# A fourth buffer for weight chunks in the FFNs of a fp32 encoder trunk, and FFN operands without the mixer's row factor

## The chip, the core and the metric

The kernel runs on one core of one Trainium2 chip. The metric is the device time of one launch in microseconds. Five engines work side by side, each on its own list of instructions in order: TensorE (PE, matmuls; PEld, its weight loads), VectorE (DVE), ScalarE (ACT), GpSimd (POOL) and SyncE (SP). Here SP and POOL do little but issue DMAs. An instruction waits on semaphores for what it needs, and everything behind it on its engine waits with it.

## The reference, cut to what matters

Two layers; in each a half-step FFN, a mixer (short convolution and chunk-band attention, gated) and a second half-step FFN; a final RMSNorm. 512 prompt frames and 8 x 16 sample frames make 640 columns.

```python
def _rmsnorm(x, g):
    y = x * lax.rsqrt(jnp.mean(x * x, axis=-1, keepdims=True) + EPS)
    return y * g

def _swiglu(h, w_gu, w_down):
    g, u = jnp.split(h @ w_gu, 2, axis=-1)          # 1024 -> 2 x 2816
    return (jax.nn.silu(g) * u) @ w_down            # 2816 -> 1024

for l in range(2):
    x = x + 0.5 * _swiglu(_rmsnorm(x, norm_ffn1[l]), w_ffn1_gu[l], w_ffn1_down[l])
    x = x + _mixer(_rmsnorm(x, norm_mix[l]), ...)
    x = x + 0.5 * _swiglu(_rmsnorm(x, norm_ffn2[l]), w_ffn2_gu[l], w_ffn2_down[l])
y = _rmsnorm(x, norm_final)
```

## The kernel before

**Layout.** x stays on the chip as 8 tiles of 128 channels by 640 columns (`x[0..7]`), in two halves of 320 columns (`HT`). Each fp32 product is made of three matmuls in a reduced fp32 form (fp32r): an operand z is split into `hi`, the rounded copy (a cast by ScalarE), and `lo = z - hi` (VectorE), and hi·hi, lo·hi and hi·lo are summed in PSUM (`multiply`, `block`).

**Weights.** They come from HBM as one stream of 379 chunks of 128 x 1024 (512 KB), `wst`, in the order of use. `load(n)` issues the DMA of chunk n on SP into a tile `raw`; the pool has three of them, so that the load of chunk n waits until chunk n-3 has been read for the last time. `prep` splits a chunk into `whi` (ScalarE, L296) and `wlo` (VectorE, L301), three buffers each. `source` makes, for the products in seven steps, sums of weight blocks (`add`, L240): first `s<-raw` and `s<-s,raw` (from the second chunk rb of a unit, and the first, ra), later `raw<-raw,raw` and `raw<-s,raw`. A unit of two chunks gives four slabs in this way. `ahead()` and `begin()` place these steps in the program in advance of the products that use them; `pending` and `flush` hold back the `lo` parts.

**FFNs.** There are four: a0, b0, a1, b1 (a before, b after the mixer of a layer; `FFNS` gives their chunks of the 22 blocks of hidden channels). `gate_up` makes one block of g and u by the seven-step scheme (`pa`, `pb`, `pc` are PSUM banks, `c_` tiles copies of them by ScalarE, called c1, u2 and c5 and held in the tag `cap` of the FFN's pool `fp`, five buffers). `down_rows` makes four output rows of the down projection of a chunk of four blocks, again in seven steps X11, X21, N6, T5, T7, 22, T4: `a` is a bank that is taken twice (after T7 by VectorE, `x<-daa` or `x<-dab`, L982; then T4 is accumulated into it and it is taken again), `b` is taken once (`x<-dba`). Other parts are staged by ScalarE into `cap` tiles (`c_a`, `u_a`) and added into x by accumulating DMAs from POOL (L977). The last chunk of an FFN goes by plain products (`pda`, `pdb`). The first blocks of a0 are made by `opening`, while x still arrives.

**Norms.** The class `Expand` makes the next FFN's operands, while the products before it still run: `final(m)` follows the last update of `x[m]`. It squares x[m] (ScalarE), multiplies x[m] by the gain g (and, in b0, a1 and b1, by the factor `rr` of the norm before, L518 on VectorE; in a0 there is none, and ScalarE does it, L516), forms sums and differences of the halves (`xe`, `xo`) and splits them. The norm's own factor `rho` isn't known yet; it is applied later to the products of the gates. With the factor `rr` in the operands, `rho` has to be the ratio of two norms: `diagonal` multiplies by `prev.s` (L587), and `inverse` makes the new `rr` (L603, in b0 alone). `total`, `root`, `diagonal` and `spread` follow in the first `gate_up`: matmuls sum the squares across channels (`nps`, L464), ScalarE takes the root, VectorE the inverse, and matmuls spread it again (`nbc`, L593).

**The room.** `sp` is a small pool that lives through the whole kernel. Its tag `rr` has two buffers of 640 columns, used by the mixer's norm (`caps` and `rr`), by `inverse`, by two tiles of `opening` and by `Final`. The pool `fp` belongs to the FFNs; it is closed before a mixer and opened again at its end. The mixer's pools `yp`, `op`, `mp` and `gp` take the same room meanwhile.

**Order.** TensorE's order is that of the program. Within `manual_schedule(engines=ORDERED)` that holds for VectorE and ScalarE too; from the block `free` of an FFN on up to its `cut`, the scheduler places VectorE's and ScalarE's instructions by its own estimate of when they are ready. SP's and POOL's queues are in order.

Of the kernel before, what the change touches and what calls it, by code (L numbers as in the profile page):

```python
# [16 lines left out]
P = 128  # L17
# [37 lines left out]

ROWS = (1, 2)

XT4, XN6, XT7, X21, X22, X11, XT5 = range(7)
# [64 lines left out]
def kinds():  # L123


    out = []

    def plain(n):
        out.extend([8] * (n // 8) + [n % 8] * (n % 8 > 0))
# [33 lines left out]
    return out  # L163

# [10 lines left out]
def trunk(ctx: ExitStack, tc: tile.TileContext, xin, wst, small, pbias, samplebias, kcache, vcache,  # L175
# [44 lines left out]
    for kind in kinds():  # L220
# [3 lines left out]
        else:  # L224
            slabs.append(("plain", n, kind * P))
            n += 1
    assert n == wst.shape[0]
    raws, ready = [], []
    sums, pool, spool = {}, [None], [None]

    def load(i):
        while len(raws) <= i:
            n = len(raws)
            raw = wp.tile([P, CH], F32, tag="raw", name=f"raw{n}", bufs=3)
            raws.append(raw)
            SP.dma_start(raw, wst[n])
        return raws[i]
# [176 lines left out]

    def norm(name, goff, ssum):

# [64 lines left out]
    class Expand(Stats):  # L481

        def __init__(self, fp, name, goff, prev):
            super().__init__(name)
            self.fp, self.goff, self.prev = fp, goff, prev
# [3 lines left out]
            self.sq = self.rest = self.rr = None  # L492
            self.known = False

        def final(self, m, square=True):
# [18 lines left out]
            B = O[:, 3:5] if odd else E[:, 0:3:2]  # L514
            if self.prev is None:
                ACT.activation(B, halves(x[m]), AF.Copy, scale=g)  # L516
            else:
                DVE.scalar_tensor_tensor(out=B, in0=halves(x[m]), scalar=g, in1=halves(self.prev.rr),  # L518
                                         op0=ALU.mult, op1=ALU.mult)
            if not odd:  # L520
# [62 lines left out]
        def diagonal(self):  # L583

            DVE.reciprocal(self.r, self.s)
            if self.prev is not None:
                DVE.tensor_tensor(out=self.r, in0=self.r, in1=self.prev.s, op=ALU.mult)  # L587
            self.turn(self.ssum, self.r)
# [10 lines left out]

        def inverse(self):  # L600

            self.rr = sp.tile([P, T], F32, tag="rr", name=f"rr{self.name}", bufs=2)
            DVE.tensor_tensor(out=self.rr, in0=self.rho, in1=self.prev.rr, op=ALU.mult)  # L603

    def opening(fp, name, goff, n, put, tails):
# [3 lines left out]
        ACT.copy(early, epst)  # L609
        ex = Expand(fp, name, goff, None)  # L610
        h = []
# [21 lines left out]
        def out(i):  # L633

            j, up = divmod(i, 2)
            if not up:
# [106 lines left out]

    def gate_up(fp, n, ex, first, turned, tails, put, j, pair, later, at):

# [125 lines left out]
        tails.append(tail)  # L871
        if first and turned:
            tails.append(ex.inverse)

# [147 lines left out]
    def ffn(name, fp, ex, goff, after, end=False):  # L1022
# [19 lines left out]
        for what, a in ffn_order(name):  # L1042
# [6 lines left out]
            if what == "gu":  # L1049
                turned = after is not None and not end  # L1050
                pair = None
                if by_seven(name, a):
                    i, odd = divmod(a - chunk_at(name, a)[0], 2)
                    if not odd:
# [3 lines left out]
                    pair = pairs[a - odd]  # L1058
                gate_up(fp, f"{name}_{a}", ex, a == plain, turned, tails, act.__setitem__, a, pair, later,
                        a - chunk_at(name, a)[0])  # L1060
# [44 lines left out]
    def mixer(l, after):  # L1105
        with tc.tile_pool(name=f"yp{l}", bufs=1, reuse_waits="tile") as yp, \
             tc.tile_pool(name=f"op{l}", bufs=1, reuse_waits="tile") as op:
            yas = yp.tile([P, CT, T], F32, name=f"ya{l}")

            h, st, stats = norm(f"m{l}", O_GM + l * KT, yas[:, 0, :])  # L1110
            rr = st.rr
# [84 lines left out]
        ex = after(st)  # L1196
        with tc.manual_schedule(engines=ORDERED):
# [450 lines left out]
    class Final:  # L1648
# [97 lines left out]
    for l in range(L):  # L1746
        if l == 0:
            open_pool("fp")
            ex = None
        ffn(f"a{l}", pool[0], ex, O_G1, None)  # L1750
        fp.close()

        def after(st):
            open_pool(f"fp{l}")
            return Expand(pool[0], f"b{l}", O_G2 + l * KT, st)

        ex = mixer(l, after)
        if l < L - 1:
            ex = ffn(f"b{l}", pool[0], ex, 0,
                     lambda: Expand(pool[0], f"a{l + 1}", O_G1 + (l + 1) * KT, ex))  # L1760
        else:
            ffn(f"b{l}", pool[0], ex, 0, Final, True)
# [135 lines left out]
```

## Time and profile before

| | us |
|---|---|
| median of 3 runs | 2515.3 |
| lowest and highest | 2515.03 and 2516.47 |
| the profiled execution, its time | 2516.73 |
| the profiled execution, its span | 2515.0 |
| granted TensorE clock, mean | 0.999 |
| weight chunks loaded by SP | 378 of 512 KB and one in four parts |
| HBM read, mean over the span | 222.70 MB |

A row of the profile names line, engine and operation, then out<-in by the program's names with their numbers left out (so `xea` and `xeb` are the tiles of the a and the b FFNs), shapes, the count, busy time, the mean of one in ns, and the idle time of the engine before it with what ended it. In order of time, the first column is the start in us from the span's start, the second the duration. The stretches of the span, as the names of the instructions show them: a0 from 0 to about 430, the first mixer to 842, b0 to 1261, a1 to 1676, the second mixer to 2087, b1 to the end at 2515.

### The profile page before, as it was taken

The page shows a single profiled execution, that of the slowest core. Times are in us where ns is not written, and L with a number is a line of the kernel's source. Part 1 is how long each engine was busy: PE and PEld are TensorE (multiplying, and loading weights), DVE is VectorE, ACT ScalarE, POOL GpSimd, SP SyncE. Part 2 cuts the span into 40 slices and gives each one's busy share as a digit, 9 for nine tenths or more (in the row PEclk, how much of TensorE's full clock was granted, in tenths as well). Part 3 has the DMA queues.
Part 4 walks back from the last instruction along what each step waited for, and adds up shares of the span by engine and source line. Part 5 has one row for each costly group of instructions (what it writes and reads, how often), then busy time and mean ns, then how long its engine had stood idle before and what let it go on. Part 6 is the DMA issues. An engine that isn't in the chain of part 4 may idle for free.

```text
span 2515.0 us, 43216 instructions
## 1 busy us (share of the span) xinstructions
PE 2495.9 (99%) x17192; PEld 2443.1 (97%) x17192; DVE 2152.0 (86%) x3471; ACT 1295.9 (52%) x2044; POOL 254.5 (10%) x377
## 2 busy tenths in 40 slices
PE   9999999999999999999999999999999999999998
PEld 8999999889999999999999999998899999999998
DVE  7889998878777998998799999988786778899997
ACT  7445556664444545555455555556644445455553
POOL 0001112112000001110001111121210000011111
PEclk9999999999999999999999999999999999999999
DMA  3233445334222234443224444453442222243444
GB/s 136 76 101 103 120 116 135 107 121 155 76 87 84 74 101 116 107 109 100 84 70 114 110 117 110 111 126 115 140 138 84 76 85 76 89 112 108 116 108 108
DMA packets 101003, 265.43 MB, mean 106 GB/s; under 512 B 11360, under 2 KB 46816, under 8 KB 100800
## 3 DMA queue, kind: packets, MB, share of 16 engines
q1 hardware_dynamic: 69408, 220.76, 27.2%
q0 software_dynamic: 30528, 41.26, 9.3%
q8 instruction: 135, 2.21, 0.4%
q10 hardware_dynamic: 864, 0.65, 0.1%
q14 instruction: 68, 0.56, 0.1%
HBM read 222.70 MB, written 7.94 MB: 92 GB/s over the span
## 4 chain that ended last, share of the span: by engine, by line
PE 79%; DVE 3%; issue 1%; ACT 1%; DMA 0%; DVEq 0%; ACTq 0%; POOLq 0%
PE pab L386 12%; PE paa L386 6%; PE pcb L386 6%; PE py L363 4%; PE po L363 4%; PE qa L386 4%; PE dab L955 4%; PE pdb L363 4%; PE pca L386 3%; PE daa L955 3%; PE pbb L386 3%; PE ma_cv L386 2%; PE pv L1397 2%; PE ma_qk L386 2%; PE qc L386 2%; PE dcb L955 2%
## 5 line engine op out<-in xcount | busy, mean ns | idle before, releaser
L296 ACT CAST whi<-raw 128x1024 fp32r<-128x1024 f32 (+1 forms) x566 | 509.4, 903 | 367.2 <-DVE raw L240 67.7
L301 DVE TENSOR_TENSOR wlo<-raw,whi 128x1024 fp32r<-128x1024 f32 (+1 forms) x566 | 585.9, 1038 | 109.8 <-ACT whi L296 107.5
L296 ACT CAST whi<-s 128x1024 fp32r<-128x1024 f32 (+1 forms) x152 | 144.4, 950 | 298.4 <-DVE s L240 170.5
L386 PE MATMUL pab<-xhib,whi 128*128 128x320 f32 x704 | 218.7, 311 | 0.5 <-ACT c_b L834 0.4
L386 PE MATMUL pab<-xhib,wlo 128*128 128x320 f32 x704 | 217.7, 309 | 0.0
L386 PE MATMUL pab<-xlob,whi 128*128 128x320 f32 x704 | 217.7, 309 | 0.0
L386 PE MATMUL paa<-xhia,whi 128*128 128x320 f32 x640 | 198.4, 310 | 1.0 <-ACT c_a L834 0.7
L386 PE MATMUL paa<-xhia,wlo 128*128 128x320 f32 x640 | 198.0, 309 | 0.0
L386 PE MATMUL paa<-xloa,whi 128*128 128x320 f32 x640 | 197.9, 309 | 0.0
L301 DVE TENSOR_TENSOR wlo<-s,whi 128x1024 fp32r<-128x1024 f32 (+1 forms) x152 | 166.0, 1092 | 5.6 <-ACT whi L296 5.6
L977 POOL DMA_DIRECT2D x<-c_b x56 | 49.2, 1017 | 1068.8 <-DVE x L982 427.8
L977 POOL DMA_DIRECT2D x<-c_a x72 | 63.4, 1021 | 836.3 <-ACT whi L296 603.8
L386 PEld LDWEIGHTS pab<-xhib,whi 128*128 128x128 f32 x704 | 132.3, 188 | 1.6 <-ACT c_b L834 0.9
L386 PEld LDWEIGHTS pab<-xlob,whi 128*128 128x128 f32 x704 | 132.3, 188 | 0.2
L386 PEld LDWEIGHTS pab<-xhib,wlo 128*128 128x128 f32 x704 | 132.3, 188 | 0.0
L386 PEld LDWEIGHTS paa<-xhia,whi 128*128 128x128 f32 x640 | 120.2, 188 | 1.6 <-ACT c_a L834 1.0
L386 PEld LDWEIGHTS paa<-xhia,wlo 128*128 128x128 f32 x640 | 120.1, 188 | 0.1
L386 PEld LDWEIGHTS paa<-xloa,whi 128*128 128x128 f32 x640 | 120.2, 188 | 0.1
L240 DVE TENSOR_TENSOR s<-raw 128x512 f32<-128x512 f32 x116 | 79.9, 689 | 45.0 <-DMA raw<-in_wst 44.6
L386 PE MATMUL pcb<-xhib,whi 128*128 128x320 f32 x352 | 108.8, 309 | 0.0
L386 PE MATMUL pcb<-xlob,whi 128*128 128x320 f32 x352 | 108.8, 309 | 0.0
L386 PE MATMUL pcb<-xhib,wlo 128*128 128x320 f32 x352 | 108.8, 309 | 0.0
(688 smaller groups left out, 8032.4 us busy)
## 6 DMA issues: line engine op xcount, KB each, us to landing
raw<-in_wst SPq DMA_DIRECT2D x378, 512.0 KB, 3.4
x<-c_a POOLq DMA_DIRECT2D x72, 160.0 KB, 3.9
x<-c_b POOLq DMA_DIRECT2D x56, 160.0 KB, 3.4
kc<-in_kcache SPq DMA_DIRECT2D x32, 256.0 KB, 3.5
vc<-in_vcache SPq DMA_DIRECT2D x16, 512.0 KB, 4.6
x<-u_a POOLq DMA_DIRECT2D x36, 160.0 KB, 4.3
x<-u_b POOLq DMA_DIRECT2D x28, 160.0 KB, 4.1
bias<-in_pbias POOLq DMA_DIRECT2D x16, 256.0 KB, 4.1
```

Source lines behind the costliest of these rows:

```text
L240: DVE.tensor_tensor(out=out, in0=a, in1=b, op=ALU.add)
L296: ACT.copy(hi[:, d], src[:, c])
L301: DVE.tensor_tensor(out=lo, in0=src, in1=hi.bitcast(F32), op=ALU.subtract)
L363: PE.matmul(ps[:, a, :HT], w, x[:, a * HT : (a + 1) * HT], start=first and j == 0, stop=last and j == 2)
L386: PE.matmul(ps, a, b, start=start and kp == 0 and j == 0, stop=stop and kp == NP - 1 and j == 2, skip_group_check=True)
L955: PE.matmul(ps[u], w, y, start=start and i == 0 and j == 0, stop=i == 1 and j == 2, skip_group_check=True)
L977: POOL.dma_start(x[ms[2 * u + r]][:, cols], z[:, u], accum_op=ALU.add)
L1397: PE.matmul(pv[t], xx[:, t * P : (t + 1) * P], w[:, kk * AW : (kk + 1) * AW], start=c == 0 and kk == 0 and j == 0, stop=c == KT // 2 - 1 a ...
```

## The change

`stages` gives the units of the stream by stage, so that the chunks inside an FFN, without its first 2 and its last 4 (`MARGIN`), are known. Of these, each fourth (n % 4 == 3) is loaded into a tile of the FFN's own pool; the others go on through the three buffers. The tag `rr` of `sp` is gone: the mixer's `caps` and `rr` lie in its pool `yp`, the opening's two tiles and the final `rr` in `cap` tiles of the FFN's pool. `Expand` has no `prev`: all FFNs' operands are x times the gain, made by ScalarE; `rho` is the norm's full factor, and `inverse` and the multiply of `diagonal` are gone.

```diff
+MARGIN = 2, 4
...
 def kinds():
-    out = []
+    return [z for _, units in stages() for z in units]
+
+def stages():
+    out, done = [], []
+
+    def end(kind):
+        done.append((kind, out[:]))
+        out.clear()
...
     for l in range(L):
         ffn(f"a{l}")
+        end("ffn")
...
         plain(held)
+        end("mixer")
         ffn(f"b{l}")
-    return out
+        end("ffn")
+    return done
...
+    inner, at = set(), 0
+    for kind, units in stages():
+        n = sum(2 if z in ("gu", "mix") else 1 for z in units)
+        if kind == "ffn":
+            inner.update(range(at + MARGIN[0], at + n - MARGIN[1]))
+        at += n
...
     def load(i):
         while len(raws) <= i:
             n = len(raws)
-            raw = wp.tile([P, CH], F32, tag="raw", name=f"raw{n}", bufs=3)
+            if n in inner and n % 4 == 3:
+                raw = pool[0].tile([P, CH], F32, tag="raw", name=f"raw{n}", bufs=1)
+            else:
+                raw = wp.tile([P, CH], F32, tag="raw", name=f"raw{n}", bufs=3)
             raws.append(raw)
             SP.dma_start(raw, wst[n])
...
-    def norm(name, goff, ssum):
+    def norm(name, goff, ssum, keep):
...
-        st.caps = sp.tile([P, T], F32, tag="rr", name=f"caps{name}", bufs=2)
-        st.rr = sp.tile([P, T], F32, tag="rr", name=f"rr{name}", bufs=2)
+        st.caps, st.rr = (keep.tile([P, T], F32, name=f"{n}{name}") for n in ("caps", "rr"))
...
-        def __init__(self, fp, name, goff, prev):
+        def __init__(self, fp, name, goff):
...
-            if self.prev is None:
-                ACT.activation(B, halves(x[m]), AF.Copy, scale=g)
-            else:
-                DVE.scalar_tensor_tensor(out=B, in0=halves(x[m]), scalar=g, in1=halves(self.prev.rr),
-                                         op0=ALU.mult, op1=ALU.mult)
+            ACT.activation(B, halves(x[m]), AF.Copy, scale=g)
...
             DVE.reciprocal(self.r, self.s)
-            if self.prev is not None:
-                DVE.tensor_tensor(out=self.r, in0=self.r, in1=self.prev.s, op=ALU.mult)
             self.turn(self.ssum, self.r)
...
-        def inverse(self):
-            self.rr = sp.tile([P, T], F32, tag="rr", name=f"rr{self.name}", bufs=2)
-            DVE.tensor_tensor(out=self.rr, in0=self.rho, in1=self.prev.rr, op=ALU.mult)
...
-            u = tmp(f"u{name}_{j}") if j > 1 else sp.tile([P, T], F32, tag="rr", name=f"u{name}_{j}", bufs=2)
+            u = tmp(f"u{name}_{j}") if j > 1 else fp.tile([P, T], F32, tag="cap", name=f"u{name}_{j}", bufs=5)
...
-        if first and turned:
-            tails.append(ex.inverse)
...
-            h, st, stats = norm(f"m{l}", O_GM + l * KT, yas[:, 0, :])
+            h, st, stats = norm(f"m{l}", O_GM + l * KT, yas[:, 0, :], yp)
...
-            rr = sp.tile([P, PARTS[0].stop], F32, tag="rr", name="frr", bufs=2)
+            rr = pool[0].tile([P, T], F32, tag="cap", name="frr", bufs=5)[:, PARTS[0]]
```

More of the change, by code (lines that the diff above doesn't have):

```diff
@@ L491, in __init__ @@
             self.ops, self.late = [], []
-            self.sq = self.rest = self.rr = None
+            self.sq = self.rest = None
             self.known = False
@@ L598, in spread @@
             self.known = True
[L600 to L603 removed]
     def opening(fp, name, goff, n, put, tails):
         ACT.copy(early, epst)
[L610 removed]
+        ex = Expand(fp, name, goff)
         h = []
@@ L742, in seven, with gate_up @@
             last(pa)
-    def gate_up(fp, n, ex, first, turned, tails, put, j, pair, later, at):
+    def gate_up(fp, n, ex, first, tails, put, j, pair, later, at):
         pa, pb, pc = (att(f"p{i}{n}")[:, :HT] for i in "abc")
@@ L1049, in ffn @@
             if what == "gu":
-                turned = after is not None and not end
                 pair = None
@@ L1058, in ffn @@
                     pair = pairs[a - odd]
-                gate_up(fp, f"{name}_{a}", ex, a == plain, turned, tails, act.__setitem__, a, pair, later,
+                gate_up(fp, f"{name}_{a}", ex, a == plain, tails, act.__setitem__, a, pair, later,
                         a - chunk_at(name, a)[0])
@@ L1195, in mixer @@
                 mo = outputs(l, gp, ops.X, st, cs, ycs, yas, sigmoid, gates)
-        ex = after(st)
+        ex = after()
         with tc.manual_schedule(engines=ORDERED):
@@ L1751, in trunk, with after @@
         fp.close()
-        def after(st):
+        def after():
             open_pool(f"fp{l}")
-            return Expand(pool[0], f"b{l}", O_G2 + l * KT, st)
+            return Expand(pool[0], f"b{l}", O_G2 + l * KT)
         ex = mixer(l, after)
@@ L1759, in trunk @@
             ex = ffn(f"b{l}", pool[0], ex, 0,
-                     lambda: Expand(pool[0], f"a{l + 1}", O_G1 + (l + 1) * KT, ex))
+                     lambda: Expand(pool[0], f"a{l + 1}", O_G1 + (l + 1) * KT))
         else:
```

2 lines of the change are left out of this document (1 added, 1 removed).

## The prediction, as it was put on record before the changed kernel ran

> **What bounds the kernel now.** I read the page's busy times first, then TensorE's waits over the whole span, then, around the longest of them, the instructions of TensorE and VectorE in order of time, and last the stage tables and the costliest groups.
>
> ```profile
> PE 2495.9 (99%) x17192; PEld 2443.1 (97%) x17192; DVE 2152.0 (86%) x3471; ACT 1295.9 (52%) x2044; POOL 254.5 (10%) x377
> ...
> raw<-in_wst SPq DMA_DIRECT2D x378, 512.0 KB, 3.4
> ```
>
> TensorE is busy for all but 19 us of a span of 2515.0 us, and its order of instructions is the same in both kernels (I compared them). So nothing that this change does can be worth more than the time in which TensorE waits inside the FFNs. Of the waits of TensorE, these lie in FFNs or at their start (total us, times, longest):
>
> ```profile
> PE daa L955 <- DVE x L982: 1.9, 3, 0.9
> ...
> PE paa L386 <- ACT c_a L834: 0.7, 1, 0.7
> ...
> PE dab L955 <- DVE x L982: 0.6, 3, 0.2
> ...
> PE pab L386 <- ACT c_b L834: 0.4, 2, 0.2
> PE pca L386 <- ACT c_a L837: 0.4, 2, 0.2
> PE paa L386 <- ACT c_a L821: 0.3, 1, 0.3
> ```
>
> That is 4.3 us in 12 waits. A wait costs more than its idle time, since a matmul is drawn longer than the step to the next one:
>
> ```profile
> 992.80 0.31 PE L955 MATMUL dcb<-ahib,wlo 128*128 128x320 f32 x1
> 993.31 0.42 PE L955 MATMUL dab<-t4hib,whi 128*128 128x320 f32 x1 [0.19 <-DVE x L982]
> 993.56 0.31 PE L955 MATMUL dab<-t4lob,whi 128*128 128x320 f32 x1
> ...
> 850.32 0.31 PE L386 MATMUL pcb<-xhib,wlo 128*128 128x320 f32 x1
> 850.47 1.24 PE L464 MATMUL npsb<-ones,ssumb 128*128 128x1 f32 x10
> ```
>
> Unhindered matmuls of 320 columns start 0.15 us apart (the last two rows). Around this wait the steps are 0.51 and 0.25, so 0.46 us is lost where the view names 0.19: 0.27 us more for each wait. The ceiling of the gain is thus 4.3 + 12 x 0.27 = 7.5 us. It has two halves: the six waits of daa and dab, 2.5 + 1.6 = 4.1 us, and the six of the gate products, 1.8 + 1.6 = 3.4 us.
>
> What makes daa wait? TensorE accumulates T4 in a bank from which VectorE must first take T7 (x<-daa). VectorE before the longest one:
>
> ```profile
> 1641.17 0.69 DVE L301 TENSOR_TENSOR wlo<-raw,whi 128x512 fp32r<-128x512 f32 x1
> 1643.56 0.69 DVE L240 TENSOR_TENSOR s<-raw 128x512 f32<-128x512 f32 x1 [1.70 <-DMA raw<-in_wst]
> ...
> 1644.90 0.68 DVE L240 TENSOR_TENSOR s<-s,raw 128x512 f32<-128x512 f32 x1
> ...
> 1646.64 0.88 DVE L982 SCALAR_TENSOR_TENSOR x<-daa,x 128x320 f32<-128x320 f32 x2
> ```
>
> VectorE stood 1.70 us for a weight chunk, with the taking of x queued behind it. Over the run:
>
> ```profile
> DVE s L240 <- DMA raw<-in_wst: 44.6, 29, 2.7
> ...
> SPq L236 <- DVE wlo L301: 2165.4, 360, 22.2
> ```
>
> The first row is VectorE waiting for chunks, the second the queue of loads waiting for VectorE to free one of three buffers. Loads are late because buffers are late; a chunk lands 3.4 us after its issue.
>
> **The fourth buffer.** In the inner chunks of each FFN a load now waits for the chunk four back instead of three. 60 of 379 chunks go to the new buffer (15 for each FFN). Bytes, issues and their order on SP stay. The scheduler, which orders VectorE and ScalarE freely inside the FFNs, answers by moving the two sums s<-raw and s<-s,raw forward. There are 32 down-projection rows (x<-dba or x<-dbb, then x<-daa or x<-dab). Before, 19 have both sums between these two takes and 2 have one. After, 1 has both (the first row of a0's last chunk, which waits now) and 9 have the second sum alone; eight of these nine had neither before. All six waits of daa and dab stand in rows that had both. Two sums are 0.69 + 0.68 us on VectorE, more than any of these waits. So all six should go but a0's, which keeps its sums and gets its chunk earlier; its part isn't more than the 1.0 us that the two shorter daa waits make together, and I leave it half of that: -4.1 + 0.5 = -3.6 us. The bounds are 0 and -4.1.
>
> The gate waits hang on copies by ScalarE, itself behind VectorE, with no DMA named: the buffer doesn't reach them. I take -0.3 us, for one multiply less in b0's second gate (rrb, below); bounds 0 and -3.4.
>
> The eight rows that gain a sum are the risk. In one of them, before:
>
> ```profile
> 1414.50 0.49 DVE L850 TENSOR_TENSOR ga<-paa,rhoa 128x320 f32<-128x320 f32 x1
> 1414.90 1.22 DVE L301 TENSOR_TENSOR wlo<-s,whi 128x1024 fp32r<-128x1024 f32 x1
> ...
> 1423.56 0.88 DVE L982 SCALAR_TENSOR_TENSOR x<-daa,x 128x320 f32<-128x320 f32 x2
> ...
> 1424.76 0.31 PE L955 MATMUL daa<-t4hia,whi 128*128 128x320 f32 x1
> ```
>
> The take ends at 1424.44 and TensorE needs it at 1424.76: 0.32 us to spare. After, both sums come ahead of it in this stretch (1.37 us), but wlo<-s (1.22 us) now stands ahead of ga<-paa,rhoa, which can't start earlier, as it waits for TensorE. Net 0.15 us later, inside the spare 0.32: I take 0. If that swap gains nothing, each row loses 1.37 - 0.32 + 0.27 = 1.3 us, eight 10.6 us. On ScalarE the cast ahia<-doa comes ahead of the taking u_a<-daa in 10 rows instead of 2, and T7 needs that taking:
>
> ```profile
> 1419.68 0.70 ACT L969 ACTIVATE u_a<-daa 128x640 f32<-128x640 f32 x1 [1.24 <-PE daa L955]
> ...
> 1421.24 0.31 PE L955 MATMUL daa<-thia,whi 128*128 128x320 f32 x1
> ```
>
> There are 0.86 us to spare here, and the two rows that had this order before show no wait: 0 us.
>
> The first use of the new room in b0 and b1 waits for a matmul of the mixer (a semaphore that these loads didn't wait for before), and all later loads are queued behind it on SP. That matmul precedes the FFN, and the loads in question are its sixth and fourth chunk: 0 us. Without that cover each of the two would be late by about one landing, 3.4 us.
>
> **The room.** caps and rr move into the mixer's pool, opened where the FFN's staging tiles (cap) lay. The mixer's sum ya therefore now waits for the last accumulating DMAs out of them:
>
> ```profile
> 1661.51 2.29 POOL L977 DMA_DIRECT2D x<-u_a  x2
> ...
> 1665.74 0.72 ACT L428 ACTIVATE ya<-x 128x640 f32<-128x640 f32 x1
> ...
> x<-u_a POOLq DMA_DIRECT2D x36, 160.0 KB, 4.3
> ...
> 1676.42 13.63 PE pv L1397 x60
> ```
>
> The second of these issues is about 1662.6 and lands near 1667, so ScalarE may stand about 1 us at ya, with the h casts behind it. TensorE is in the plain products of the FFN's end until 1676.42, when pv first needs these casts, so 0 us; if that cover were gone, 1 us for each mixer. The opening's two u tiles and the final rr in cap tiles add no instruction: 0 us.
>
> **Operands from x times the gain alone.** In three FFNs VectorE's x·g·rr becomes ScalarE's x·g; b0's rr product and three tiny products go.
>
> ```profile
> L516 ACT ACTIVATE xoa<-x,sm 128x640 f32<-128x640 f32 x4 | 3.3, 828 | 0.3 <-DVE xloa L551 0.3
> ...
> L518 DVE SCALAR_TENSOR_TENSOR xob<-x,sm,rrm 128x640 f32<-128x640 f32 x8 | 7.0, 881 | 0.1
> ...
> L603 DVE TENSOR_TENSOR rrb<-rhob,rrm 128x640 f32<-128x640 f32 x1 | 0.8, 818 | 0.0
> L587 DVE TENSOR_TENSOR ninvb<-ninvb,nrmsm 128x5 f32<-128x5 f32 x2 | 0.3, 167 | 0.1
> ...
> 791.00:842.00 51.00, 51.00 (x349) 51.00 (x349) 41.27 (x55) 20.32 (x25) 0.00 (x0) 1.00 0.19 63
> ```
>
> 24 x 0.88 us leave VectorE and 24 x 0.83 us come to ScalarE (its form is there in a0). The last row is a stage in which they fall (PE, PEld, VectorE, ScalarE busy of 51 us): TensorE is full, and ScalarE goes from 20.3 to 20.3 + 8 x 0.83 = 27 us. Seven of eight of them are hidden under the products, either way: 0 us. The eighth is not, since TensorE runs into the first gate with little left to cover it:
>
> ```profile
> 842.16 0.82 DVE L1203 TENSOR_TENSOR x<-po,x 128x640 f32<-128x640 f32 x1
> 843.02 0.88 DVE L518 SCALAR_TENSOR_TENSOR xob<-x,sm,rrm 128x640 f32<-128x640 f32 x1
> 843.94 0.49 DVE L529 SCALAR_TENSOR_TENSOR xob<-xeb,xob 128x320 f32<-128x320 f32 x1
> ...
> 848.63 1.68 DVE L240 TENSOR_TENSOR ssumb<-ssumb,sqb 128x640 f32<-128x640 f32 x2
> ...
> 843.02 0.74 ACT L570 ACTIVATE sqb<-x 128x640 f32<-128x640 f32 x1 [0.35 <-DVE x L1203]
> 843.66 0.41 ACT L768 COPY c_b<-pab 128x320 f32<-128x320 f32 x1
> ```
>
> Before, xob runs on VectorE beside the square on ScalarE. After, it stands behind the square, from 843.66 to 844.49, so xob<-xeb starts at 844.55 instead of 843.94: 0.61 us late. VectorE's chain from there to the sums of squares is tight; they end at 850.31 + 0.61 = 850.92, and TensorE, which reaches npsb at 850.47, stands 0.45 us. Three such places: +1.4 us. The bounds are +0.3 (0.1 each) and +2.5 (0.83 each). The tiny product that goes behind npsb (0.17 us) frees nothing, as TensorE's own T7 products fill that time.
>
> The Trainium skill speaks against this move: in ScalarE: Activation LUTs, section Rules for kernel authors, it says to use VectorE and not ScalarE for a multiply. Its section What ACT_TABLE_LOAD costs gives 186 ns + 0.833 ns per element and 93 ns for a pointer operand, an estimate of 812 ns here; by it the sum would be the same within 0.1 us, and the rows (828 against 881) show no slower ScalarE for this form.
>
> **Sum.** -3.6 - 0.3 + 1.4 = -2.5 us. The profiled execution took 2516.7 (span 2515.0 and 1.7 around it), so it would take 2514.2. It lies 1.4 above the median of the runs, 2515.3, so the median becomes 2512.8.
>
> **Rivals.**
> (a) All waits go: VectorE, with 0.88 us less at each step and no DMA stops, also clears the gates, and the last operand finds its cover. -7.5 + 0.3 = -7.2: 2508.1. For it: all waits hang on VectorE or on what it feeds. Against: the gate waits show no DMA before them.
> (b) The transfers were hidden anyway: VectorE's 44.6 us of DMA waits shrink but TensorE gains nothing, since 29 such waits stand against six of daa and dab. +1.4: 2516.7.
> (c) Slower: the sums moved ahead of x<-daa make the eight rows late. +10.6 + 1.4 - 3.6 = +8.4: 2523.7. It decides as soon as VectorE comes to that take more than 0.32 us later than now; for it speaks that VectorE has no pause in that row.
> (d) ScalarE paces the operands, all 24 on the path: 24 x 0.83 = +19.9, 2535. The stage row (27 of 51 us) speaks against it. The skill's rule named above would point this way.
>
> **How the numbers follow.** Chances: forecast 0.50, (a) 0.25, (b) 0.08, (c) 0.15, (d) 0.02. 0.2% is 5 us, about what a measurement of this kernel can tell from no change. Faster by more: (a) and the forecast's lower edge, 0.28. Slower by more: (c), (d) and a little of (b), 0.18. Within: 0.54. The forecast's own range is 2510.5 to 2516; the range for 8 in 10 takes in (a) and (b) and the nearer half of (c): 2507.5 to 2521.
>
> **What would show it.** Right: VectorE's waits for raw fall from 44.6 to under 15 us, TensorE's waits daa/dab on x to one or two, and new waits npsa/npsb of about 0.3 us on the sum of squares appear three times. Wrong: waits of daa or dab in the first row of a chunk, eight of them; or pauses of TensorE in the first gates unchanged while daa keeps its 1.9 us; or a long wait of ScalarE at ya that reaches pv.

## The result, and the profile after

| | median, us | lowest and highest | runs |
|---|---|---|---|
| before | 2515.89 | 2514.16 to 2517.84 | 20 |
| after | 2512.18 | 2511.21 to 2512.65 | 20 |

The ratio of the times is 0.9985, with a 95% interval of 0.9979 to 0.9991: 3.7 us less, and at least 2.3. The profiled execution took 2511.21 us, its span is 2509.4 (before: 2516.73 and 2515.0). The runs also lie closer together, within 1.4 us of each other and not 3.7.

The page of after, busy times of the engines:

```profile
PE 2492.8 (99%) x17192; PEld 2441.8 (97%) x17192; DVE 2127.2 (85%) x3443; ACT 1322.0 (53%) x2068; POOL 253.9 (10%) x377
```

VectorE has 25 us less and ScalarE 26 us more. The 24 operands that moved, with the instructions that went, are some 20 of these on either engine (ops_alone, below, has -20.4 and +17.3). TensorE's own work is the same; what changed is its gaps. TensorE's waits in the FFNs, after (total us, times, longest):

```profile
PE paa L410 <- ACT c_a L845: 0.7, 1, 0.7
...
PE pca L410 <- ACT c_a L848: 0.4, 2, 0.2
PE paa L410 <- ACT c_a L832: 0.3, 1, 0.3
PE dab L964 <- DVE x L991: 0.2, 1, 0.2
```

The three waits of daa are gone, and of dab's three one is left. VectorE's waits, after:

```profile
DVE s L264 <- DMA raw<-in_wst: 5.1, 6, 1.4
```

Of 44.6 us in 29 waits for chunks, 5.1 us in 6 are left. The place of the longest daa stop, VectorE in order of time, after:

```profile
1633.57 0.68 DVE L264 TENSOR_TENSOR s<-raw 128x512 f32<-128x512 f32 x1
...
1636.04 0.68 DVE L264 TENSOR_TENSOR s<-s,raw 128x512 f32<-128x512 f32 x1
1636.65 0.88 DVE L991 SCALAR_TENSOR_TENSOR x<-dba,x 128x320 f32<-128x320 f32 x2
...
1641.95 0.88 DVE L991 SCALAR_TENSOR_TENSOR x<-daa,x 128x320 f32<-128x320 f32 x2
```

Both sums now run ahead of x<-dba, with no wait in front of them, and x<-daa comes 5.3 us after x<-dba. Before, it came 7.0 us after (1639.64 to 1646.64):

```profile
1639.64 0.89 DVE L982 SCALAR_TENSOR_TENSOR x<-dba,x 128x320 f32<-128x320 f32 x2 [0.18 <-PE dba L955]
```

**Where TensorE's time went.** For the table I add up, over all matmuls, the time from the start of one to the start of the next, by the bank that the next one writes, and subtract the same sum of before's profiled execution. So each number is what that kind of product gained or lost, in us, waits and drawn-out steps together.

| | rows (da, db, dc) | gates (pa, pb, pc) | sums of squares (npsa, npsb) | spread (nbca, nbcb) | all else | all |
|---|---|---|---|---|---|---|
| after | -4.35 | -0.43 | +0.36 | -0.34 | -0.75 | -5.50 |
| after, run again (changed_again) | -4.41 | -0.40 | +0.37 | -0.33 | -0.80 | -5.57 |
| ops_alone | -2.02 | +0.53 | +0.37 | -0.34 | -0.21 | -1.67 |
| buffer_in_b | -3.18 | -0.26 | +0.37 | -0.33 | +0.16 | -3.25 |
| buffer_vector | -4.30 | -0.41 | -0.21 | -0.34 | -0.55 | -5.80 |
| last_vector | -4.18 | -0.71 | -0.21 | -0.34 | -0.27 | -5.71 |
| last_twice | -4.28 | +2.75 | +0.37 | -0.34 | +0.19 | -1.30 |
| sums_first | +1.87 | +6.45 | -0.01 | 0.00 | -0.05 | +8.25 |

"All else" is mostly the start and the mixers. Between kernels that differ in neither it lies anywhere from -0.8 to +0.2, so its -0.75 is not put down to the change. Before's execution was itself 0.8 to 1.4 us slower than its medians, and those of after and changed_again were 1.0 and 0.8 us faster than theirs; the medians say 3.4 to 3.7 us.

### The profile page after: what moved, and what is told of

Same layout as the page of the kernel before. It is cut to its first block, busy times and chain, and to the rows that moved or that the text cites. A ratio compares the mean times of both kernels' runs of the same rounds, so it can differ in the third digit from the quotient of the medians.

```text
span 2509.4 us, 43302 instructions
## 1 busy us (share of the span) xinstructions
PE 2492.8 (99%) x17192; PEld 2441.8 (97%) x17192; DVE 2127.2 (85%) x3443; ACT 1322.0 (53%) x2068; POOL 253.9 (10%) x377
## 4 chain that ended last, share of the span: by engine, by line
PE 96%; DVE 2%; issue 1%; ACT 1%; DMA 1%; SPq 0%; DVEq 0%; ACTq 0%; POOLq 0%
PE pab L410 12%; PE paa L410 11%; PE pcb L410 6%; PE pca L410 6%; PE daa L964 5%; PE py L387 4%; PE po L387 4%; PE qa L410 4%; PE dab L964 4%; PE pdb L387 4%; PE pbb L410 3%; PE pba L410 3%; PE dca L964 3%; PE ma_cv L410 2%; PE pda L387 2%; PE pv L1405 2%
## 5 line engine op out<-in xcount | busy, mean ns | idle before, releaser
L264 DVE TENSOR_TENSOR raw<-raw,raw 128x512 f32<-128x512 f32 x152 | 103.7, 682 | 0.5
```

The costliest lines, as they stand in the source:

```text
L264: DVE.tensor_tensor(out=out, in0=a, in1=b, op=ALU.add)
```

## The experiments

Twelve kernels, in three sets. The kernel before ran beside each set: 2515.41, 2515.51 and 2515.32 us.

| kernel | median, us | lowest and highest | ratio to before, 95% |
|---|---|---|---|
| ops_alone | 2515.08 | 2514.88 to 2517.18 | 1.0000 (0.9992 to 1.0009) |
| buffer_vector | 2510.98 | 2510.65 to 2511.92 | 0.9982 (0.9973 to 0.9991) |
| last_vector | 2511.12 | 2510.77 to 2511.60 | 0.9982 (0.9974 to 0.9991) |
| sums_first | 2524.94 | 2524.47 to 2526.05 | 1.0038 (1.0025 to 1.0052) |
| buffer_in_b | 2513.57 | 2513.06 to 2516.20 | 0.9994 (0.9985 to 1.0003) |
| last_twice | 2515.40 | 2514.58 to 2516.26 | 1.0000 (0.9991 to 1.0009) |
| tails_late | 2523.19 | 2522.43 to 2524.43 | 1.0029 (1.0018 to 1.0041) |
| late_and_vector | 2523.10 | 2520.55 to 2523.93 | 1.0027 (1.0017 to 1.0038) |
| changed_again | 2511.88 | 2511.10 to 2512.39 | 0.9986 (0.9977 to 0.9995) |
| last_vector_again | 2511.26 | 2510.47 to 2511.78 | 0.9983 (0.9974 to 0.9992) |
| cast_late | 2511.87 | 2511.65 to 2512.49 | 0.9987 (0.9978 to 0.9996) |
| cast_and_vector | 2511.00 | 2510.47 to 2512.77 | 0.9984 (0.9975 to 0.9993) |

### The operands and the room without the buffer

ops_alone is the changed kernel with three buffers everywhere. The sums of weight blocks then stand where they stood before (19 of 32 rows hold both).

```diff
-            if n in inner and n % 4 == 3:
-                raw = pool[0].tile([P, CH], F32, tag="raw", name=f"raw{n}", bufs=1)
-            else:
-                raw = wp.tile([P, CH], F32, tag="raw", name=f"raw{n}", bufs=3)
+            raw = wp.tile([P, CH], F32, tag="raw", name=f"raw{n}", bufs=3)
```

> The changed kernel with three buffers for all chunks; operands from x times the gain, and the room, stay as changed. Its order on VectorE is that of before but for the instructions that the change drops. Theory (the fourth buffer makes the gain, by the sums that leave the rows): TensorE's six waits daa/dab on x come back (2.5 us, six times), VectorE's waits for raw are near 44.6 us again, the time is that of before within 1.5 us. Rival (the lighter VectorE makes the gain): the six waits stay away or shrink below 1 us and the time is within 1 us of the changed kernel's.

It took 2515.08 us, no change against before that can be measured. VectorE waited for chunks for 42.3 us, 28 times. TensorE's waits in its rows:

```profile
PE dab L961 <- DVE x L988: 0.6, 3, 0.2
...
PE dba L961 <- DVE x L988: 0.4, 2, 0.2
...
PE daa L961 <- DVE x L988: 0.2, 1, 0.2
```

So the time is the theory's, but of the six stops of daa and dab four come back, with 0.8 us. Daa's waits are 0.2 us here and were 1.9 before, with the same order of the sums. VectorE at the same place as before's longest stop, in ops_alone:

```profile
1641.59 0.69 DVE L261 TENSOR_TENSOR s<-raw 128x512 f32<-128x512 f32 x1 [0.18 <-DMA raw<-in_wst]
1642.29 0.83 DVE L228 TENSOR_TENSOR aloa<-ua,ahia 128x640 fp32r<-128x640 f32 x1
...
1644.83 0.88 DVE L988 SCALAR_TENSOR_TENSOR x<-daa,x 128x320 f32<-128x320 f32 x2
```

The chunk came 0.18 us late in this execution and 1.70 in before's. From issue to landing it took 4.78 us in before and 3.27 in ops_alone; the traces of buffer_in_b and sums_first, which have three buffers at this place too, show 3.39 and 3.21. The other long stop, in a0 at 403 us, has the same story: 4.59 us in before, 3.42 to 3.46 in the other three, and no stop of daa there in any of them. So the two long stops that I took as the kernel's, 2.23 us with their drawn-out steps, were one execution's draw of how long two chunks take to land; why these two took longer isn't known. In the medians the operands' move and the room are worth -0.3 us, and the buffer, from ops_alone to after, -2.9 (2515.08 to 2512.18; -3.2 to changed_again, and 3.1 to 3.4 if each is read against the kernel before beside it). In the traces that is rows -2.33 and gates -0.96.

The four stops that are left in ops_alone are the short ones of before, 0.46 us each with the drawn-out step, and no late chunk makes them. Before, in b0, around the one at 1141.6 us:

```profile
1136.39 0.69 DVE L240 TENSOR_TENSOR s<-raw 128x512 f32<-128x512 f32 x1 [0.29 <-DMA raw<-in_wst]
1137.12 0.69 DVE L240 TENSOR_TENSOR s<-s,raw 128x512 f32<-128x512 f32 x1
1138.26 0.82 DVE L214 TENSOR_TENSOR alob<-ub,ahib 128x640 fp32r<-128x640 f32 x1 [0.45 <-ACT ahib L213]
1139.53 1.23 DVE L301 TENSOR_TENSOR wlo<-raw,whi 128x1024 fp32r<-128x1024 f32 x1 [0.45 <-ACT whi L296]
1140.67 0.88 DVE L982 SCALAR_TENSOR_TENSOR x<-dab,x 128x320 f32<-128x320 f32 x2
```

Behind the sums VectorE waits for two casts of ScalarE, and the split wlo<-raw, which needs the second of them, stands ahead of the take. In the changed kernel both sums have left this row, and the stop is still there, 0.46 us at 1138.3:

```profile
1134.97 0.83 DVE L228 TENSOR_TENSOR alob<-ub,ahib 128x640 fp32r<-128x640 f32 x1 [1.30 <-ACT ahib L227]
1136.24 1.23 DVE L325 TENSOR_TENSOR wlo<-raw,whi 128x1024 fp32r<-128x1024 f32 x1 [0.44 <-ACT whi L320]
1137.38 0.88 DVE L991 SCALAR_TENSOR_TENSOR x<-dab,x 128x320 f32<-128x320 f32 x2
```

The other three (205, 993 and 2257 us before) are gone in the changed kernel, and in these rows the scheduler has put the split behind the take. The one at 993, before and after:

```profile
991.23 1.23 DVE L301 TENSOR_TENSOR wlo<-raw,whi 128x1024 fp32r<-128x1024 f32 x1 [0.17 <-ACT whi L296]
992.37 0.88 DVE L982 SCALAR_TENSOR_TENSOR x<-dab,x 128x320 f32<-128x320 f32 x2
```

```profile
988.60 0.89 DVE L991 SCALAR_TENSOR_TENSOR x<-dab,x 128x320 f32<-128x320 f32 x2 [0.54 <-PE dab L964]
...
989.88 1.21 DVE L325 TENSOR_TENSOR wlo<-raw,whi 128x1024 fp32r<-128x1024 f32 x1
```

Nine rows of the kernel before have both sums but the split behind the take, and none of them stops.

### The buffer in two FFNs of four

```diff
         ffn(f"b{l}")
-        end("ffn")
+        end("b")
...
-        if kind == "ffn":
+        if kind == "b":
             inner.update(range(at + MARGIN[0], at + n - MARGIN[1]))
```

> The changed kernel with its fourth buffer in the b FFNs alone; a0 and a1 load through three. Theory (the buffer acts where it stands: the sums of weight blocks come ahead of the rows' takes again in a0 and a1): in a0 and a1 TensorE again stops at daa, dab or dba, 1 to 2.5 us together with the drawn-out steps, and VectorE waits there for raw about 20 us; in b0 and b1 the rows lose at most 0.3 us and VectorE waits for raw at most 4 us. The time lies between the two, 2512 to 2513.5. Rival (one FFN's buffer, or its new order of loads, works on through the whole stream; the two that had the long stops, a0 and a1, are helped by the rest): rows lose about 1 us in all and the time is that of the changed kernel, 2511 to 2511.8.

It took 2513.57 us, just above the theory's 2512 to 2513.5 and 1.4 to 1.7 us above the changed kernel. VectorE's waits for chunks over the whole run:

```profile
DVE s L264 <- DMA raw<-in_wst: 21.0, 15, 2.4
```

Of these, 9.4 us (6 waits) lie in a0 and 7.4 (4) in a1; 0.6 (1) in b0 and 2.5 (2) in b1. The rows lose 1.2 us against the changed kernel, and in b0 and b1 every stop is the changed kernel's. So the buffer acts in the FFN in which it stands.

### More sums ahead of the takes

sums_first is the kernel before with the two sums moved forward by priority: 29 of 32 rows now hold both between the two takes, not 19. It is the mechanism of my rival (c), with no buffer to soften it.

```diff
+                    with tc.high_priority(offset=300):
-                    add(st[:, h2], rb[:, h1], rb[:, h2])
-                    add(st[:, h1], st[:, h2], ra[:, h1])
+                        add(st[:, h2], rb[:, h1], rb[:, h2])
+                        add(st[:, h1], st[:, h2], ra[:, h1])
```

> The kernel before with its three buffers, but the two sums s<-raw and s<-s,raw given a higher priority in the scheduler. With three buffers this puts both sums between the takes of b and a in 29 of 32 rows (19 before). Theory (sums that wait for a late chunk ahead of x<-daa make TensorE stop): waits daa/dab rise from 6 to 10 or more and the time rises by 1 to 6 us. Rival (the place of the sums doesn't matter): waits daa/dab stay 6, the time that of before.

It took 2524.94 us, 9.5 more than before; the theory had 1 to 6. TensorE's waits in it:

```profile
PE paa L387 <- DVE ga L240: 2.0, 4, 0.8
PE daa L956 <- DVE x L983: 1.4, 7, 0.2
PE dab L956 <- DVE x L983: 1.2, 6, 0.2
```

VectorE waits for chunks for 65.9 us now, 38 times. There are 13 stops of daa and dab where before had six. The count is the theory's, but not its cause: in 12 of the 13 rows VectorE waits for no chunk between the takes (in the other 0.28 us), and in all 13 the split wlo<-raw, behind a wait for ScalarE's cast, stands ahead of the take, as in the short stops above. The row at 1448 us shows it: in sums_first it has no wait for a chunk but the split ahead of the take, and loses 0.46 us; before, at 1443, it has both sums and a wait of 0.48 us for a chunk but the split behind the take, and loses nothing. A sum placed ahead of its chunk stops TensorE in two rows, with waits of 0.77 and 0.58 us for the chunk, by 0.35 and 0.16 us; these are too short for the view. The larger loss, 6.45 of 8.25 us in the table, is in the gates: VectorE's ga<-paa, late in the same queue, holds the bank that the next products want. The longest of these stops, 0.8 us at 1329.5, comes behind a wait of 1.07 us for a chunk at 1325.8, with no pause of VectorE between. The same path shows in the kernel before, in b0:

```profile
942.99 0.49 DVE L240 TENSOR_TENSOR gb<-pab,c_b 128x320 f32<-128x320 f32 x1
943.09 0.31 PE L386 MATMUL pcb<-xhib,wlo 128*128 128x320 f32 x1
...
943.53 0.41 PE L386 MATMUL pab<-xhib,whi 128*128 128x320 f32 x1
```

TensorE should go on at 943.24 (0.15 after 943.09), and starts at 943.53, as VectorE leaves the bank at 943.48. 16 us earlier (at 927.3) VectorE had stood 0.4 us for a chunk, and from there to 943.48 it has no pause; in ops_alone that wait is 0.7 us and this stop 0.3 us longer; in the changed kernel both are gone.

### The last operand

Three kernels vary the operand of m = 7 alone or with the others. last_twice lets ScalarE make it twice:

```diff
             ACT.activation(B, halves(x[m]), AF.Copy, scale=g)
+            if square and end:
+                ACT.activation(B, halves(x[m]), AF.Copy, scale=g)
```

> The changed kernel in which ScalarE makes the operand of m = 7 twice in b0, a1 and b1 (the same values into the same place), so that what follows it comes another 0.83 us later. Theory (TensorE's stop at npsa/npsb follows the last operand one to one, and 0.1 us was left of it only because VectorE's take x<-po came 0.6 us or more earlier than in the kernel before): each of the three stops grows by 0.7 to 0.83 us, together 2.1 to 2.5 us, time 2513 to 2514. Rival (the sums of squares have slack of their own, and the 0.1 us stops belong to something else): the stops grow by less than 0.3 us each, time below 2512.3.

It took 2515.40 us, 3.2 to 3.5 more than the changed kernel and above both expectations. So this chain is tight, 1.1 us for each 0.83 us, more than the theory's one to one. But the stop isn't where the theory and I had put it. TensorE in order of time with what it waits for, last_twice in b0:

```profile
846.10 1.16 DVE L571 TENSOR_TENSOR xlob<-xob,xhib 128x960 fp32r<-128x960 f32 x1 [0.33 <-ACT xhib L556]
...
847.18 1.22 DVE L325 TENSOR_TENSOR wlo<-raw,whi 128x1024 fp32r<-128x1024 f32 x1
847.32 0.41 PE L410 MATMUL pab<-xlob,whi 128*128 128x320 f32 x1 [0.38 <-DVE xlob L571]
...
848.32 1.68 DVE L264 TENSOR_TENSOR ssumb<-ssumb,sqb 128x640 f32<-128x640 f32 x2
...
848.45 0.42 PE L410 MATMUL pcb<-xhib,wlo 128*128 128x320 f32 x1 [0.28 <-DVE wlo L325]
```

The last operand's low part is needed by the products pab<-xlob, and the split of the next weights stands behind it on VectorE. Both stop TensorE ahead of npsb, whose own 0.1 us is unchanged (+0.37 in the table). The sums of squares come behind them and gain from each stop.

last_vector has that one operand made by VectorE, buffer_vector all 24 (`not square` in place of the condition):

```diff
-            ACT.activation(B, halves(x[m]), AF.Copy, scale=g)
+            if not square or not end:
+                ACT.activation(B, halves(x[m]), AF.Copy, scale=g)
+            else:
+                DVE.tensor_scalar(out=B, in0=halves(x[m]), scalar1=g, scalar2=None, op0=ALU.mult)
```

> The changed kernel with the last operand alone (m = 7) of b0, a1 and b1 on VectorE, the other seven on ScalarE. Theory (the 0.61 us behind the square is real, and most of it was paid by the relief upstream): both stops of TensorE (0.11 us each) go at three places, -0.6 us. Rival (the stop has another cause): TensorE stops as in the changed kernel.

> The changed kernel with x times the gain on VectorE instead of ScalarE in b0, a1 and b1 (one source, without the row factor); the fourth buffer stays. Theory (the buffer makes the gain, and ScalarE at the last operand costs a little): the rows' waits stay away, TensorE's stop ahead of the three sums of squares (0.11 us and 0.11 us just before it) goes or shrinks to under 0.1 us; time as the changed kernel's or up to 0.7 us less. Rival (VectorE's relief of 0.88 us at each step is needed): VectorE is behind again at the last x update, TensorE stops up to 0.5 us at each of the three places, time 1 to 3 us more.

> The changed kernel itself, beside the next three on one chip, so that differences below 1 us are read against it. Expected 2511.5 to 2512.5, and in its trace the same two 0.1 us stops in each of b0, a1 and b1 (at the weights' split, then at npsa/npsb). The pause of VectorE that made the longest daa stop of the kernel before depends on one chunk's landing; with the fourth buffer nothing hangs on it, so the runs should lie within 1.5 us of each other, against some 3 us for the kernel before.

> The operand of m = 7 made by VectorE in b0, a1 and b1, a second time, beside the changed kernel. Theory (the last operand behind the square costs two stops of 0.22 us together, in three places): 0.5 to 0.8 us under the changed kernel. Rival (the difference between calls was the chip's): within 0.3 us of it.

Beside each other on one chip the changed kernel took 2511.88 (changed_again, its runs within 1.3 us of each other, as expected) and last_vector 2511.26 us (last_vector_again): 0.6 us for the three places, inside the 0.5 to 0.8 expected. In its trace the stops at the weights' split and at npsa/npsb are gone; the three stops behind ScalarE's copies in the second gates (861.6, 1280.7 and 2103.4 us in last_vector) grow by 0.05 us each. buffer_vector, 2510.98, can't be told from last_vector: the other 21 operands are hidden on either engine. So ScalarE's queue is not what the operands wait for, rival (d), except at the last one.

### The gates that are left

Four kernels tried for the stops that stay at the second gates, 0.9 us in a1 and 0.4 us in b0 and b1. In the ordered gates, tails_late puts all the last steps of the gate before (multiply, cast, split) behind ScalarE's copy u2, and cast_late only the cast and its subtraction; late_and_vector and cast_and_vector are each of them with last_vector's operand. `late` is true for a gate whose order is that of the program (`a < free`).

```diff
-            for t in tails:
-                t()
-            tails.clear()
+            if not late:
+                for t in tails:
+                    t()
+                tails.clear()
...
             ACT.copy(u2, pa)
+            if late:
+                for t in tails:
+                    t()
+                tails.clear()
+                flush()
```

```diff
+            casts[0] = [] if late else None
             for t in tails:
                 t()
             tails.clear()
+            held, casts[0] = casts[0] or [], None
...
             ACT.copy(u2, pa)
+            for t in held:
+                t()
...
-            ACT.copy(halves(hi), z[:, at])
-            self.low(halves(lo), halves(hi), z[:, at])
+
+            def cast():
+                ACT.copy(halves(hi), z[:, at])
+                self.low(halves(lo), halves(hi), z[:, at])
+
+            if casts[0] is None:
+                cast()
+            else:
+                casts[0].append(cast)
```

> The changed kernel in which, in the gates whose order is that of the program (the first of an FFN), the last steps of the gate before (its multiply and its splits) come behind ScalarE's second copy u2 instead of ahead of it. Theory (the gate waits that are left are this order's: ScalarE's copy stands behind the gate before, not behind any weight chunk): the stops at paa and pca at 861, 1281 and 2103 us go or halve, 0.7 to 1.5 us, time 2509.7 to 2510.5. Rival (the stop moves on to the next copy or to the gate's own splits, which the down projection needs): the gates lose as much as before or more, time 2511 to 2513.

> The one before, with the operand of m = 7 made by VectorE in b0, a1 and b1. If the stops at npsa/npsb and those of the first gates are separate, the gains add up: 0.4 to 0.7 us from the first beside what the late tails give alone, and the time is the lowest of all, 2509 to 2510. If the multiply on VectorE (0.55 us) comes back at the copies of the first gate, no more than the late tails alone give.

> The changed kernel in which, in the ordered gates, only ScalarE's cast ahi of the gate before (and VectorE's subtraction behind it) comes behind the copy u2; the multiplies stay where they were. The kernel with all the last steps behind u2 lost 2 us in each of these gates, at the copy behind the weights' casts. Theory (the stop before the last products of the second gates, 0.9 us in a1 and 0.4 us in b0 and b1 with the drawn-out step, is the cast of 0.73 us that stands before u2): these stops fall by 1.0 to 1.7 us together, time 2510.5 to 2511.2. Rival (the late subtraction, or the copy c5 behind the cast, stops TensorE instead): 2512 or more.

> Both: the late cast and the last operand on VectorE. If the two are separate, 1.5 to 2.4 us under the changed kernel, 2509.7 to 2510.6, the lowest of all; if the cast only moves the stop, the time of the kernel with the last operand on VectorE alone.

tails_late took 2523.19 us, 11 us more than the changed kernel: both theory and rival missed by far. u2 came in time, but the copy behind it, c5, now stood behind the cast of the late steps, and TensorE stopped for 1.9 to 2.2 us in each of three gates. And that wasn't all. Windows of tails_late in b0 (length, busy us of PE, PEld, VectorE, ScalarE, POOL with counts, granted clock, DMA share, GB/s):

```profile
860.00:865.00 5.00, 3.73 (x26) 3.46 (x24) 4.43 (x6) 3.01 (x5) 0.00 (x0) 1.00 0.41 135
865.00:868.00 3.00, 2.36 (x12) 1.96 (x12) 2.93 (x6) 0.77 (x3) 0.00 (x0) 0.83 0.33 130
868.00:870.50 2.50, 2.49 (x9) 2.49 (x10) 2.08 (x4) 0.71 (x1) 0.00 (x0) 0.52 0.00 0
870.50:875.00 4.50, 4.50 (x33) 4.50 (x32) 2.31 (x3) 2.54 (x4) 0.00 (x0) 1.00 0.00 0
```

After the stop, which ended at 865.5, the granted clock fell to half: 0.50 over the stretch from 867.0 to 870.4, and in the third row nine matmuls in 2.5 us where 17 fit. Of the three stops two are followed by such a fall (here and at 2112.8); the longest, 2.2 us at 1288.6, is not. The rest of the 10.4 us that the gates lose in this trace are the stops themselves, 6.0 us, and later ones at paa and pab behind VectorE. With last_vector's operand on top (late_and_vector) it is 2523.10, the same within the scatter of the runs.

cast_late took 2511.87 us, the changed kernel's time; its rival came nearer. In a1:

```profile
PE paa L410 <- DVE wlo L325: 0.7, 2, 0.4
```

The waits on ScalarE's copies (0.7 and 0.3 us) are gone there, and the weights' split on VectorE stops TensorE for nearly as much: 1.27 us with the drawn-out steps, in place of 1.50. In b0 and b1 the stops are unchanged, so they hang on something else, which wasn't tried. cast_and_vector, 2511.00, isn't below last_vector by more than the runs scatter.

**The lowest times** are those of the changed kernel with the last operand or all of them on VectorE (cast_and_vector among them), 2511.0 to 2511.3 us; against the changed kernel in the same set that is 0.6 to 0.9 us less.

## Why the prediction was right, and where it wasn't

The forecast was 2512.8, the median came out at 2512.18. That is nearer than the sum was, and by luck: the forecast started from 2515.3, the median of three runs, and 20 runs of the same kernel have 2515.89. The sum was -2.5 us; the medians moved by -3.7. On the profiled execution the same terms measure -4.8, of which 2.2 are the draw of before's execution. Term by term:

- **Rows, -3.6: measured -4.35.** The six stops that were counted gave -3.61 with their drawn-out steps, so the number came out, but the mechanism holds for two of them alone.
  The two long ones (403 and 1647 us, 2.23 us together) were VectorE's wait for a chunk, handed on through x<-daa, as predicted; but they belong to one execution, and ops_alone, with before's order of the sums, lost 2.02 us less in the rows than before did.
  Three short ones (1.38 us) went because the split wlo<-raw moved behind the take, which the prediction did not have. The step that failed for these: "two sums are 0.69 + 0.68 us, more than any of these waits, so all six should go but a0's". Behind the sums VectorE waited for ScalarE, so that taking them out gains nothing by itself: the fourth short stop (1141.6, now 1138.3) lost both sums and kept its 0.46 us. And a0's first row of the last chunk, which was to keep a stop, loses nothing at daa. That five of six went, as forecast, is luck in part.
  Outside the count, 0.42 us came from two stops of 0.21 (180 and 2232 us), too short for the view of waits, whose rows lost both sums, and 0.32 from dba: after the long daa stops the next products lost 0.41 us each at 407 and 1651, and lose 0.24 and 0.26 now (404.7 and 1646.8). To quote a stop of 0.94 us from one trace, I would have needed a bound for what the landing does to it.
- **The eight rows that gain a sum, 0: right.** None of the nine rows that hold the second sum has a stop. sums_first shows that the risk was real, by 0.35 and 0.16 us in the two rows where the chunk was 0.77 and 0.58 us late.
- **Gates, -0.3: measured about -0.75** (-0.43 in the table and 0.32 that the last operand costs in the same banks). The step that failed: "the buffer doesn't reach them". The gates wait for VectorE's queue as the rows do, only further behind the wait; the stop at 943 us is that, 0.41 us with its drawn-out step, and 0.10 us at 1356.6 went with the buffer too (ops_alone and buffer_in_b keep it). What I had counted, the product rrb in b0, gave 0.20: before, TensorE loses that at 872.7 us, behind gb<-pab at 871.1, and VectorE's queue has no pause from rrb (865.0) to there; ops_alone has the same order without rrb, VectorE pauses 0.40 us at that place, and TensorE doesn't stop.
- **The last operand, +1.4: measured +0.7** (npsa/npsb +0.36, and three stops of 0.11 at the weights' split). Right mechanism, wrong size. I held the start of its chain fixed at before's x<-po; but the same change takes the multiply of 0.88 us off VectorE at m = 6, ahead of it, and puts a wait of 0.40 us for ScalarE's operand in its place. After, in b0, in order of time:

```profile
838.29 1.21 DVE L325 TENSOR_TENSOR wlo<-s,whi 128x1024 fp32r<-128x1024 f32 x1
...
839.56 0.82 DVE L1211 TENSOR_TENSOR x<-po,x 128x640 f32<-128x640 f32 x1
...
840.42 0.74 ACT L588 ACTIVATE sqb<-x 128x640 f32<-128x640 f32 x1
...
841.07 0.81 ACT L537 ACTIVATE xob<-x,sm 128x640 f32<-128x640 f32 x1
...
841.91 0.49 DVE L547 SCALAR_TENSOR_TENSOR xob<-xeb,xob 128x320 f32<-128x320 f32 x1 [1.53 <-ACT xob L537]
...
846.61 1.68 DVE L264 TENSOR_TENSOR ssumb<-ssumb,sqb 128x640 f32<-128x640 f32 x2
846.75 0.42 PE L410 MATMUL pcb<-xhib,wlo 128*128 128x320 f32 x1
...
848.43 1.25 PE L487 MATMUL npsb<-ones,ssumb 128*128 128x1 f32 x10
```

  The lateness is there: VectorE stands 1.53 us for xob. But x<-po starts 8.87 us ahead of npsb and not 8.31 as before (842.16 to 850.47). Of these 0.56 us, 0.22 are the two stops themselves, and 0.34 an earlier start, which pays that much of the 0.61.
- **The tiny product behind npsb, 0: measured -0.34**, 0.11 in each of three places (nbc). All kernels with the new operands have it and sums_first, with the old ones, does not; so the T7 products did not hide that product after all.
- **The room and the queue, 0: right.** ScalarE goes into ya without a pause, and among SP's waits for its loads no wait on a matmul shows. ScalarE's operands were hidden, seven of eight, as costed.

Of what I named to look for: VectorE's waits for chunks are under 15 us (5.1), of daa and dab one is left; the stops at npsa/npsb came three times, at 0.11 and not 0.3 us. Rival (b) falls by the medians, with -2.9 us or more from ops_alone to after, and (d) by buffer_vector; (a) is out because gates keep 1.4 us of waits, (c) because none of the rows that gained a sum stops.

Three things stay open: why two chunks took longer to land in before's execution; why the stops of the second gates in b0 and b1 did not move with the cast; and how the buffer's worth is shared between chunks that land earlier and the order that the scheduler makes of it. No kernel has the new order with three buffers, or the old order with four, and whether the split moved because the sums left isn't shown. The traces put 1.38 of the 2.33 us in the rows on the order of the split, and on a late chunk the 0.7 us that ops_alone loses in the gates at 943 us.

## What to carry to other kernels

A wait for a load on an engine that works in order costs whatever stands behind it in the queue: look at the rows behind the wait, the gates as well as the next take, and don't count its own microseconds, 39.5 of which went here for some 3. See too whether the engine waits again, for another engine, ahead of the instruction that matters: then the first wait costs nothing there, as in the four short stops, and the order of what stands between decides. When you cost a step that becomes late, move the start of its chain by what the same change takes off ahead of it, and follow the chain to its first consumer. A stop that hangs on when a transfer lands needs more than one execution before its size goes into a sum.

## What was not expected of the hardware

The multiply by a gain takes 0.55 us on VectorE when it reads one tensor in SBUF, and 0.88 when it reads two. The operand's instruction in after (ScalarE) and in buffer_vector (VectorE), min, median and max in ns:

```profile
L537 ACT ACTIVATE xob<-x,sm x8: 813/817/822, 798.8 to 2082.9; 128x640 f32<-128x640 f32 x8
```

```profile
L540 DVE TENSOR_SCALAR xob<-x,sm x8: 546/548/554, 799.2 to 2082.0; 128x640 f32<-128x640 f32 x8
```

On ScalarE it takes 0.82. The Trainium skill has the gain of the one-tensor form, in VectorE: DVE Perf Modes, section The perf-mode tier table (the rule you actually need): with one source in SBUF, fp32 too runs at twice the rate of two sources. The trace agrees in the direction, not in the size: 548 against 881 ns is 1.6 times and not twice, for whole instructions of 640 elements. I had weighed ScalarE against the old form only, and did not ask what VectorE would take for the new one.

Stops of about 2 us halved the granted clock, but not each time. In tails_late two of three stops were followed, 0.5 to 1.5 us after their end, by 3.41 us at a granted clock of 0.50 (from 867.0 and from 2112.8 us, after stops of 1.9 us); the longest, 2.2 us at 1288.6, was not. In late_and_vector it was the stops at 865 and 1288 us, and not the one at 2113. A stop of 1.1 us (before, at 1647.6) did not draw out any but the next step. The Trainium skill, in TensorE: Matmul & The Clock Gate, Part 1, has the clock fall after an idle window of about 3.4 us that runs free of the kernel. By the runs here less was enough in four of six cases: an idle time of 1.8 to 2.2 us. What decides when it is enough isn't shown.
